# A decoder layer in split fp32: twelve of 22 feed-forward tiles go through the second weights in Strassen's form

## The chip, the cores and the metric

The kernel runs on one core of one Trainium2 chip. The metric is the device time of one execution in microseconds (us). A core has TensorE (PE) for matmuls into PSUM banks, VectorE (DVE), ScalarE (ACT) and GpSimd (POOL) for elementwise work, and SyncE (SP), whose queue issues the DMA transfers of this kernel in order.

## The reference, cut to what matters

One layer of a decoder for 1024 prompt tokens and 8 sample tokens: attention and convolution branches, their merge, then a SwiGLU feed-forward part and a gated per-layer embedding. All is float32. The change is in the feed-forward part, which computes, for the normed input h of all 1032 tokens,

```python
x = x + rms_norm(swiglu(rms_norm(x)))        # D_MODEL = 1024, D_FF = 2816
# swiglu(h): g, u = h @ w_ffn_in (1024 x 2*2816);  (silu(g) * u) @ w_ffn_out (2816 x 1024)
```

## The kernel before, in words

Activations lie transposed: features on 128 partitions, T = 1032 tokens along the free axis. D = 1024 features are KT = 8 tiles, the hidden width 2816 is NH = 22 tiles. Each float32 product is made of three matmuls: an operand is split by ScalarE, which copies it to a rounded "hi" tile, and by a subtraction that leaves the rest in a "lo" tile; `mm3` (lines 277 to 280) multiplies hi by hi, hi by lo and lo by hi into one bank. Tokens are taken in three chunks of 344 (`LC`) or in four quarters of 258 (`QN`).

The feed-forward part has two stages. The hidden stage makes tile after tile of silu(g)·u. Tiles 0 to 2 are plain products (`hidden_plain`). From tile 3 (`CLASSIC`) on it uses Strassen's form: `prepare(j)` makes sums of the four quarters of the weights on POOL and splits them, `token_sums(p)` has made four sums of quarters of h for each token half p on VectorE ahead of the stage, and a `Quad` runs seven products per token half in place of eight, in the order 1, 2, 6, 5, 7, 3, 4 (`ORDER`), over three banks. The hidden values are gathered in a slot `pk` and stored to DRAM (`d_h`), one slot and one store per tile and token half.

The second weights' stage multiplies the hidden tiles with w_ffn_out. It takes the 22 tiles in five groups, `HID = (4, 4, 3, 5, 6)`. For each group, `load_hidden` reads a tile back from `d_h` (`hr`) and splits it into `uh` (ScalarE) and `ul` (VectorE); the weights are loaded (`raw`) and split into `wh` and `wl`. For each chunk and each of the 8 output tiles f, `ffn_out` accumulates the group in one bank, and VectorE copies or adds it into `fac[f]` (`fa` in the profile). Loads for the next group go on beside the group in hand. The last group runs chunk by chunk with the final norm and the embedding behind it (`last_chain`, `p_bank`).

What sets the order: the program is written in order per engine, and a scheduler of the tile framework then moves instructions by priorities and estimated times. Tiles come from pools: `act` from 43 large slots, `raw` from 3, `sc` from 4, `rl` from 6; a tile waits until its slot's former readers are done. Banks come in turn from seven. `copies` are cache rows copied from DRAM to DRAM on SP's queue between other work. Generators that are advanced by `next(...)` between products, such as `prepare`, put side work among the matmuls.

Of the kernel before, what the change touches and what calls it, by code (L numbers as in the profile page):

```python
# [10 lines left out]
F32 = mybir.dt.float32  # L11
# [40 lines left out]
LAG = 2  # L52
TL = 2
TP = 2
HID = (4, 4, 3, 5, 6)


@with_exitstack
def decoder_step(ctx: ExitStack, tc: tile.TileContext, ins, outs):
# [24 lines left out]
    def act(s, dt=F32):  # L84
        return actp.tile([P, SLOT], dt, tag="act", name=nm(s))
# [4 lines left out]
    def rl(s):  # L90
        return rlp.tile([P, CW], F32, tag="rl", name=nm(s))
# [48 lines left out]
    def scratch(name, shape):  # L140
        return dram.tile(list(shape), F32, name=name)
# [39 lines left out]
    def w_rows(w, k):  # L181
        wq.append((w[k * P:(k + 1) * P, :].rearrange("p (f m) -> p f m", m=P), 8))
        return len(wq) - 1

    raws = {}

    def load_weight():
        j = w_emitted[0]
        src, n = wq[j]
        r = rawp.tile([P, 8 * P], F32, tag="raw", name=nm("raw"))  # L190
        SY.dma_start(r[:, :n * P].rearrange("p (k m) -> p k m", m=P), src)
        raws[j] = r
        w_emitted[0] += 1

# [22 lines left out]
    def W(i):  # L217
        return wt[i]
# [194 lines left out]
    wi_ff, h0 = [], 0  # L413
    for n_ in HID:
        wi_ff.append([w_rows(w_ffn_out, h0 + j) for j in range(n_)])
        h0 += n_
# [840 lines left out]
    def token_sums(p):  # L1257


        for j in range(4):  # L1260
            tsum[p][j] = act("th", F32R), act("tl", F32R)
        for k in range(4):
            b11, b12, b21, b22 = (m_q(f, 2 * p + h) for f in (k, k + 4) for h in range(2))
            t = [rl("t") for _ in range(4)]
            for x, a, b in ((0, b12, b11), (2, b22, b12), (1, b22, 0), (3, b21, 1)):
                V.tensor_sub(t[x][:, :QN], a, t[b][:, :QN] if isinstance(b, int) else b)
# [56 lines left out]
    prods = {}  # L1323

    def prepare(j):


        a, b = fetch(wi_st[j]), fetch(wi_st[j] + 1)
        H = 4 * P
        a1, a2, b1, b2 = a[:, :H], a[:, H:], b[:, :H], b[:, H:]  # L1330
        w = prods[j] = {}

        def split(src, hi, lo):
            A.activation(hi, src, AF.Copy)
# [10 lines left out]
        G.tensor_add(s1, b1, b2)  # L1345
        G.tensor_sub(s2, s1, a1)
# [6 lines left out]
        G.tensor_sub(s3, a1, b1)  # L1353
# [4 lines left out]
        G.tensor_sub(s4, a2, s2)  # L1358
# [11 lines left out]
    class Quad:  # L1370


        def __init__(self, j, p):
            self.j, self.p, self.t0 = j, p, 2 * p * QN
            self.banks, self.part = {}, {}
            self.pk = act("pk")

        def piece(self, i):
            return self.pk[:, i * QN:(i + 1) * QN]

        def operand(self, m, k):
            quarter = {1: (0, 0), 2: (4, 0), 3: (4, QN)}
# [15 lines left out]
        def after(self, m):
# [24 lines left out]
            else:  # L1423
                V.tensor_mul(x, ps, x)

    def hidden_strassen(j, nxt):
        for group in ((0,), (1,)) if j == CLASSIC else ((0, 1),):
            quads = []
            for p in group:
                finish(2)  # L1430
                finish(("t", p))
                quads.append(Quad(j, p))
# [6 lines left out]
            for q in quads:  # L1439
                SY.dma_start(d_h[j, :, q.t0:q.t0 + 2 * QN], q.pk[:, :2 * QN])  # L1440
        del prods[j]

    for js, qs in [(range(2), range(2)), ((2,), (0,)), (range(2), (2,)), ((2,), (1, 2))]:
        for j in js:
            ensure(wi_cl[j][1])
            for q in qs:
                hidden_plain(j, q)
    hid = {}

    def load_hidden(j):  # L1450
# [3 lines left out]
        V.tensor_sub(lo, r, hi.bitcast(F32))  # L1454
        hid[j] = hi, lo

    def first_hidden():
        for _ in range(2):
            yield
        for j in range(HID[0]):  # L1460
            ensure(wi_ff[0][j])
            yield
            load_hidden(j)
            yield

    prep = prepare(CLASSIC)
    for j in range(CLASSIC, NH):
# [10 lines left out]

    fac = [None] * KT

    def ffn_out(gi, h0, wo, f, c):
        t0, n = c
        ps = gemm_bank_rows(wo, f, [hid[h0 + k] for k in range(len(wo))], c)
        if fac[f] is None:
            fac[f] = act("fa")
        fv = fac[f][:, t0:t0 + n]
        if gi == 0:
            V.tensor_copy(fv, ps[:, :n])
        else:
            V.tensor_add(fv, fv, ps[:, :n])  # L1490

    h0 = 0
    for gi, wo in enumerate(wi_ff[:-1]):
        nj, nh = h0 + len(wo), h0 + len(wo) + len(wi_ff[gi + 1])
        nw = wo[-1] + 1
        for ci, c in enumerate(LC):
            for f in range(KT):
                ffn_out(gi, h0, wo, f, c)
                if f % 3 == 2 and nj < nh:
                    ensure(nw)  # L1500
                    load_hidden(nj)
                    nj, nw = nj + 1, nw + 1
                elif f % 4 == 3:
                    next(copies, None)
        h0 += len(wo)
    wo, gi = wi_ff[-1], len(wi_ff) - 1
    rbs = [None] * 3

    hp = [None] * 3
# [22 lines left out]
    for ci, c in enumerate(LC):  # L1532
        accs[ci] = SumSq(c)
        nf = KT - LQ if ci == 2 else KT
        for f in range(nf):
            ensure(wo[-1])
            ffn_out(gi, h0, wo, f, c)
            accs[ci].add(f, fac[f][:, c[0]:c[0] + c[1]])
            tick(2.9)
        if nf < KT:  # L1540

            t0, n = c
            pss = [bank() for f in range(nf, KT)]
            for k, wi in enumerate(wo):
                (wh, wl), (xh, xl) = W(wi), hid[h0 + k]
# [148 lines left out]
```

## Time and profile before

| | |
|---|---|
| three runs | 1713.76, 1708.15, 1712.81 us |
| median | 1712.81 us |
| the profiled execution's own time | 1709.87 us |
| its span, first to last instruction | 1708.1 us |
| mean granted TensorE clock | 0.997 |
| hidden stage, Strassen tiles (3 to 21) | about 936 to 1335 us of the span |
| second weights' stage with its last group | about 1340 to 1590 us |

In rows of the profile, a line such as "fa<-fa,g 128x344" names the written tile, the read tiles and the shape; g is a PSUM bank. All elementwise work stands under L120, a helper that records it, so it is told apart by tile names. Two times beside a row of the timeline are its start and its duration in us; square brackets hold how long the engine sat idle before it and what ended that. Matmul rows overlap: the time that one takes from the engine is the distance from start to start.

### The profile page before, as it was taken

To read this page: it belongs to the slowest core of one execution; us is meant where nothing else is said; L and a number is where in the kernel's file an instruction comes from. 1 tells how busy PE (TensorE), PEld (TensorE's weight loads), DVE (VectorE), ACT (ScalarE), POOL (GpSimd) and SP (SyncE) were. 2 spreads that over 40 slices of the span, in tenths; PEclk is the share of its full clock that TensorE was granted. 3 is DMA by queue.
4 is the path that set the end of the run, shared out by engine and by line. 5 is a ranking of instruction groups with operands and counts; after the bars stand their busy time and mean duration, and the time that the engine had idled before them with its cause. 6 is when DMAs were issued, how large, how long until landed. Compare 5 with 4: busy or idle time off the path is not lost.

```text
span 1708.1 us, 28632 instructions
## 1 busy us (share of the span) xinstructions
PE 1681.4 (98%) x11651; PEld 1653.5 (97%) x11651; DVE 1036.4 (61%) x1742; ACT 634.0 (37%) x1307; POOL 288.9 (17%) x223
## 2 busy tenths in 40 slices
PE   8999999999999999999999999999999999999999
PEld 7999999999999999999999989999999999999998
DVE  7899879958979677553789312222212445637863
ACT  6434445444442344223544333333333311213520
POOL 1000000000000000000004666766664000000000
PEclk9999999999999999999999999999999999999999
DMA  5242121121254355323331222333333523420411
GB/s 190 64 124 66 43 67 57 49 82 62 89 180 156 112 179 157 106 81 107 127 117 42 73 87 87 100 117 103 109 99 124 186 108 103 171 96 13 149 59 46
DMA packets 80890, 174.65 MB, mean 102 GB/s; under 512 B 11154, under 2 KB 49890, under 8 KB 80374
## 3 DMA queue, kind: packets, MB, share of 16 engines
q1 hardware_dynamic: 80566, 172.69, 31.0%
q8 instruction: 91, 1.49, 0.4%
q0 software_dynamic: 192, 0.13, 0.1%
q14 instruction: 41, 0.34, 0.1%
HBM read 136.16 MB, written 50.13 MB: 109 GB/s over the span
## 4 chain that ended last, share of the span: by engine, by line
PE 88%; DVE 6%; issue 2%; DMA 1%; ACT 1%; POOL 1%; SPq 0%; POOLq 0%; DVEq 0%; ACTq 0%
PE g L278 28%; PE g L280 28%; PE g L279 28%; DVE y L120 3%; PE O L675 1%; PE S L630 1%; PE PT L657 1%; DVE tl L120 1%; DVE t L120 1%; DMA d_h<-pk 1%; DVE wl L120 1%; POOL s L120 0%; DMA hr<-d_h 0%; PE m L337 0%; PE m L325 0%
## 5 line engine op out<-in xcount | busy, mean ns | idle before, releaser
L278 PE MATMUL g<-hh,wh 128*128 128x384 f32 (+1 forms) x1200 | 393.3, 328 | 7.1 <-ACT wh L120 7.1
L280 PE MATMUL g<-hh,wl 128*128 128x384 f32 (+1 forms) x1200 | 384.5, 321 | 0.3 <-DVE wl L120 0.3
L279 PE MATMUL g<-hl,wh 128*128 128x384 f32 (+1 forms) x1200 | 384.1, 320 | 0.0
L120 DVE SCALAR_TENSOR_TENSOR y<-z,taps,y 128x1023 f32<-128x1023 f32 (+14 forms) x240 | 304.0, 1267 | 36.7 <-ACT y L120 31.1
L278 PEld LDWEIGHTS g<-hh,wh 128*128 128x128 f32 x1200 | 226.6, 189 | 14.4 <-ACT wh L120 7.1
L279 PEld LDWEIGHTS g<-hl,wh 128*128 128x128 f32 x1200 | 226.4, 189 | 0.6 <-DVE hl L120 0.3
L280 PEld LDWEIGHTS g<-hh,wl 128*128 128x128 f32 x1200 | 226.0, 188 | 0.8 <-DVE wl L120 0.8
L279 PE MATMUL g<-ul,wh 128*128 128x344 f32 x528 | 169.4, 321 | 0.0
L280 PE MATMUL g<-uh,wl 128*128 128x344 f32 x528 | 168.7, 321 | 0.0
L278 PE MATMUL g<-uh,wh 128*128 128x344 f32 x528 | 162.2, 321 | 3.3 <-ACT uh L120 3.3
L120 DVE TENSOR_TENSOR wl<-raw,wh 128x1024 fp32r<-128x1024 f32 x106 | 129.1, 1222 | 35.6 <-ACT wh L120 28.7
L120 POOL TENSOR_TENSOR r<-r,mhalf 128x3 f32<-128x3 f32 x18 | 16.4, 910 | 752.8 <-DVE r L120 752.7
L120 ACT ACTIVATE wh<-raw 128x1024 fp32r<-128x1024 f32 x106 | 110.7, 1050 | 8.0 <-PE g L279 3.8
L278 PE MATMUL g<-mh,wh 128*128 128x344 f32 x336 | 107.6, 323 | 0.8 <-ACT mh L120 0.8
L120 DVE TENSOR_TENSOR pk<-p,g 128x258 f32<-128x258 f32 x76 | 31.0, 421 | 126.5 <-PE g L280 97.8
L279 PE MATMUL g<-ml,wh 128*128 128x344 f32 x336 | 107.1, 320 | 0.0
L280 PE MATMUL g<-mh,wl 128*128 128x344 f32 x336 | 107.0, 320 | 0.0
L278 PEld LDWEIGHTS g<-uh,wh 128*128 128x128 f32 x528 | 98.2, 189 | 3.6 <-ACT uh L120 3.6
L279 PEld LDWEIGHTS g<-ul,wh 128*128 128x128 f32 x528 | 99.7, 189 | 0.4 <-DVE ul L120 0.4
L120 DVE TENSOR_TENSOR p<-p,g 128x258 f32<-128x258 f32 x38 | 16.1, 425 | 138.1 <-ACT p L120 77.2
L280 PEld LDWEIGHTS g<-uh,wl 128*128 128x128 f32 x528 | 99.7, 189 | 0.0
L120 DVE TENSOR_TENSOR fa<-fa,g 128x344 f32<-128x344 f32 x96 | 47.1, 511 | 78.3 <-PE g L280 77.9
(236 smaller groups left out, 4034.1 us busy)
## 6 DMA issues: line engine op xcount, KB each, us to landing
raw<-in_w_in_dram SPq DMA_DIRECT2D x50, 512.0 KB
raw<-in_w_ffn_in_dram SPq DMA_DIRECT2D x44, 512.0 KB
hr<-d_h SPq DMA_DIRECT2D x22, 516.0 KB
raw<-in_w_ffn_out_dram SPq DMA_DIRECT2D x22, 512.0 KB
d_h<-pk SPq DMA_DIRECT2D x38, 258.0 KB
out_kvs_dram<-in_cache_kv_w_dram SPq DMA_DIRECT2D x16, 510.0 KB
d_x<-mo SPq DMA_DIRECT2D x24, 172.0 KB
out_yT_dram<-fa SPq DMA_DIRECT2D x24, 172.0 KB
```

The lines of the kernel that those rows point to most:

```text
L120: ins = fn(*a, **k)
L278: TE.matmul(ps, hi_w, xh, start=first, stop=False, skip_group_check=more)
L279: TE.matmul(ps, hi_w, xl, start=False, stop=False, skip_group_check=more)
L280: TE.matmul(ps, lo_w, xh, start=False, stop=last, skip_group_check=more)
L630: TE.matmul(sp[h][:, o:o + nk], qT[h * 64:(h + 1) * 64, blk * P:(blk + 1) * P], kT[h * 64:(h + 1) * 64, (blk + 1) * P - nk:(blk + 1) * P], ...
L657: TE.transpose(ps[:, o:o + P], e[:, o:o + P], ident)
L675: TE.matmul(ps[h * 64:(h + 1) * 64, i * P:(i + 1) * P], vtok[:, k0:k0 + 64], self.p[half][:, o:o + P], start=kb == kbs[0], stop=kb == kbs[-1])
```

## The change

Tiles 0 to 3 and 16 to 21 stay plain in the second stage. Tiles 4 to 15 become six pairs; in a pair the two tiles are the two halves of the sum index. The two token quarters of a token half and the two halves of the output rows are the other halves, so a pair takes seven products of 258 columns in place of eight. Two pairs (`PER`) are summed in a bank before it is added to the `fa` tiles that the product goes into; VectorE adds the running bank after each product, in place of a copy per part.

- Weights: `w_pair` loads one half of the output columns for both tiles of a pair, with two transfers. `mix_weights` makes four sums and all splits' subtractions on POOL: 16 instructions for a half of two pairs. In the stage of before POOL has no work.
- Hidden values: `hidden_store` makes, after each odd tile, four sums per token half on VectorE (`ts`) and stores the seven operands' sources to a new DRAM scratch `d_s`. `mix_hidden` reads them back (two transfers per pair and token half) and splits them: ScalarE the hi part, VectorE the subtractions (7 for two pairs).
- `pk` is now one slot per tile for both token halves, held until the pair is stored.
- The first part's banks are moved to `fa` by ScalarE, not VectorE.
- In the hidden stage `token_sums` makes three split sums, not four. The fourth overwrites a quarter of `mo` and is split later into `h2` by `fourth_sums`. The preparation of tile 3 has its sums and subtractions on VectorE, not POOL. The last tile is run one token half after the other.

```diff
-HID = (4, 4, 3, 5, 6)
+PLAIN0, PAIRS, PER = 4, 6, 2
...
-        for j in range(4):
+        for j in range(3):
             tsum[p][j] = act("th", F32R), act("tl", F32R)
...
+                if x == 3:
+                    V.tensor_sub(b12, a, b)
+                    continue
+                V.tensor_sub(t[x][:, :QN], a, b)
...
+    def fourth_sums(p):
+        for k in range(4):
+            src = m_q(k, 2 * p + 1)
+            hi, lo = (y[:, (2 * p + 1) * QN:(2 * p + 2) * QN] for y in h2[k])
+            A.activation(hi, src, AF.Copy)
+            V.tensor_sub(lo, src, hi.bitcast(F32))
+            yield 0.35
...
     def prepare(j):
+        E = V if j == CLASSIC else G
...
-            G.tensor_sub(lo, src, hi.bitcast(F32))
+            E.tensor_sub(lo, src, hi.bitcast(F32))
...
+    def hidden_store(j, p):
...
+        i, e = divmod(j - PLAIN0, 2)
+        d = d_s[i, p]
+        if e == 0:
+            SY.dma_start(d[:, 4 * QN:5 * QN], pk[:, t0:t0 + QN])
+            return
+        SY.dma_start(d[:, 5 * QN:], pk[:, t0:t0 + 2 * QN])
...
+        V.tensor_sub(t1, b12, b11)
+        V.tensor_sub(t2, b22, t1)
+        V.tensor_sub(t3, b22, b12)
+        V.tensor_sub(t4, b21, t2)
+        SY.dma_start(d[:, :4 * QN], ts)
...
-        for group in ((0,), (1,)) if j == CLASSIC else ((0, 1),):
+        for group in ((0,), (1,)) if j in (CLASSIC, NH - 1) else ((0, 1),):
...
-            V.tensor_copy(fv, ps[:, :n])
+            A.activation(fac[f][:, t0:t0 + n], ps[:, :n], AF.Copy)
...
+    def mix_weights(g, half):
...
+            split(a1, *direct[0], G)
+            split(r[:, 2 * H:], *direct[1], G)
+            yield
+            G.tensor_add(s1, b1, b2)
+            G.tensor_sub(s2, s1, a1)
+            split(sa, hi[:, :2 * H], lo[:, :2 * H], G)
+            yield
+            G.tensor_sub(s3, a1, b1)
+            G.tensor_sub(s4, a2, s2)
+            split(sb, hi[:, 2 * H:4 * H], lo[:, 2 * H:4 * H], G)
...
+    def mix_hidden(g, p):
+        rest = [act("ux", F32R) for _ in range(3)]
+        for e in range(PER):
+            d = d_s[g * PER + e, p]
+            rb, rt = act("hr"), act("hr")
+            SY.dma_start(rb[:, :3 * QN], d[:, 4 * QN:])
+            SY.dma_start(rt, d[:, :4 * QN])
...
+    class OutQuad:
...
+        def product(self, m):
...
+            for e in range(PER):
...
+                mm3(ps, QN, wh, wl, xh, xl, e == 0 and m in OPENS, e == PER - 1, m not in OPENS)
+            c = {1: self.c11, 2: self.c11, 6: self.c12, 3: self.c12, 5: self.c22, 7: self.c22, 4: self.c21}[m]
+            V.tensor_add(c, c, ps)
...
+            ahead = [mix_hidden(g, 1), mix_weights(g + 1, 0), mix_hidden(g + 1, 0), mix_weights(g + 1, 1)]
...
+        for (p, half), nxt in zip(((0, 0), (0, 1), (1, 0), (1, 1)), ahead):
+            for _ in pre:
+                pass
+            pre = nxt
+            quads = [OutQuad(g, p, half, i) for i in range(2)]
+            for m in ORDER:
+                for q in quads:
+                    q.product(m)
+                    next(pre, None)
```

The new part runs as twelve blocks of 84 matmuls, called B0 to B11: three groups of two pairs, in each group the blocks (token half 0, output half 0), (0, 1), (1, 0), (1, 1). `split` in the new functions is a hi copy on ScalarE and a subtraction on the engine given last (G is POOL, V is VectorE).

Three places show how the instructions now stand. First VectorE in the second stage. Before, in the first group, copies of finished banks alternate with splits for the next group:

```order
L120 COPY fa_13981<-g_13968 128x344
L120 COPY fa_13996<-g_13983 128x344
L120 TENSOR_TENSOR wl_14001<-raw_13829,wh_14000 128x1024
L120 COPY fa_13966<-g_14099 128x344
L120 TENSOR_TENSOR ul_14006<-hr_14004,uh_14005 128x1032
L120 COPY fa_14023<-g_14010 128x344
L120 COPY fa_14039<-g_14026 128x344
```

After, at the end of B1 and the start of B2 (ux and usl are the splits that B2 needs, hr what was read back):

```order
L120 TENSOR_TENSOR fa_14142<-fa_14142,g_14588 128x258
L120 TENSOR_TENSOR fa_14164<-fa_14164,g_14610 128x258
L120 TENSOR_TENSOR ux_14465<-hr_14467,ux_14464 128x774
L120 TENSOR_TENSOR usl_14490<-hr_14468,ush_14489 128x516 x2
L120 TENSOR_TENSOR ux_14465<-hr_14502,ux_14464 128x258
L120 TENSOR_TENSOR ux_14466<-hr_14502,ux_14466 128x516
L120 TENSOR_TENSOR fa_14010<-fa_14010,g_14734 128x258
L120 TENSOR_TENSOR fa_14039<-fa_14039,g_14749 128x258
L120 TENSOR_TENSOR fa_14010<-fa_14010,g_14759 128x258
L120 TENSOR_TENSOR usl_14525<-hr_14503,ush_14524 128x516 x2
```

Five splits stand directly behind B1's last adds, and two more behind the third add of B2.

Second, POOL at the same place, where it had no row before; these belong to the weights of B4 and B6 (sums sa and sb, splits wx):

```order
L120 TENSOR_TENSOR sa_14604<-raw_14261 128x256
L120 TENSOR_TENSOR sb_14605<-raw_14261 128x256
L120 TENSOR_TENSOR sa_14604<-sa_14604,raw_14261 128x256
L120 TENSOR_TENSOR sb_14605<-raw_14261,sa_14604 128x256
L120 TENSOR_TENSOR sa_14647<-raw_14322 128x256
L120 TENSOR_TENSOR sb_14648<-raw_14322 128x256
L120 TENSOR_TENSOR sa_14647<-sa_14647,raw_14322 128x256
L120 TENSOR_TENSOR sb_14648<-raw_14322,sa_14647 128x256
L120 TENSOR_TENSOR wx_14597<-raw_14261,wx_14596 128x256
```

POOL now has a row of 16 such instructions for every half of two pairs, one after the other.

Third, VectorE ahead of the hidden stage's tile 3, among the sums for token half 1 (t, tl). Before:

```order
L120 TENSOR_TENSOR t_9308<-mo_7705 128x258
L120 TENSOR_TENSOR t_9310<-mo_7709,mo_7705 128x258
L120 TENSOR_TENSOR tl_9221<-t_9268,th_9220 128x258
L120 TENSOR_TENSOR t_9309<-mo_7709,t_9308 128x258
L120 TENSOR_TENSOR tl_9215<-t_9308,th_9214 128x258
```

After, at the end of the same sums, with the preparation of tile 3 (s, wal, wbl) among them:

```order
L120 TENSOR_TENSOR mo_7706<-mo_7710,t_9234 128x258
L120 TENSOR_TENSOR t_9273<-mo_7707 128x258
L120 TENSOR_TENSOR wal_9399<-raw_9019,wah_9398 128x1024
L120 TENSOR_TENSOR tl_9175<-t_9273,th_9174 128x258
L120 TENSOR_TENSOR t_9275<-mo_7711,mo_7707 128x258
L120 TENSOR_TENSOR t_9274<-mo_7711,t_9273 128x258
L120 TENSOR_TENSOR wbl_9407<-s_1258_9403,wbh_9406 128x512
```

The instructions wal, wbl and s stood in POOL's row before; the fourth sum is written into mo and its split has left this place.

More of the change, by code (lines that the diff above doesn't have):

```diff
@@ L183, in w_rows, with w_pair @@
         return len(wq) - 1
+    def w_pair(w, ks, half):
+        srcs = [w[k * P:(k + 1) * P, :].rearrange("p (b h c) -> p b h c", b=2, h=2)[:, :, half] for k in ks]
+        wq.append((srcs, None))
+        return len(wq) - 1
     raws = {}
@@ L412, in decoder_step @@
         w_cols(w_ffn_in, DFF + j * P)
[L413 to L416, printed above, removed]
+    pairs = [(PLAIN0 + 2 * i, PLAIN0 + 2 * i + 1) for i in range(PAIRS)]
+    LAST0 = PLAIN0 + 2 * PAIRS
+    wi_ff = {j: w_rows(w_ffn_out, j) for j in range(PLAIN0)}
+    wi_fs = {}
+    for g in range(0, PAIRS, PER):
+        for half in range(2):
+            for i in range(g, g + PER):
+                wi_fs[i, half] = w_pair(w_ffn_out, pairs[i], half)
+    for j in range(LAST0, NH):
+        wi_ff[j] = w_rows(w_ffn_out, j)
     wi_P = [w_cols(w_ple_gate, i * P) for i in range(NPG)]
@@ L1344, in prepare @@
         s1, s2 = sc("s1"), sc("s2")
-        G.tensor_add(s1, b1, b2)
-        G.tensor_sub(s2, s1, a1)
+        E.tensor_add(s1, b1, b2)
+        E.tensor_sub(s2, s1, a1)
         w[6], w[5] = halves(act("wbh", F32R), act("wbl", F32R))
@@ L1424, in after @@
                 V.tensor_mul(x, ps, x)
+    packs = {}
+    def hidden_store(j, p):
+        t0 = 2 * p * QN
+        pk = packs[j]
+        if not PLAIN0 <= j < LAST0:
+            SY.dma_start(d_h[j, :, t0:t0 + 2 * QN], pk[:, t0:t0 + 2 * QN])
+            return
[3 more added lines that the diff above has]
+            SY.dma_start(d[:, 4 * QN:5 * QN], pk[:, t0:t0 + QN])
+            return
+        SY.dma_start(d[:, 5 * QN:], pk[:, t0:t0 + 2 * QN])
+        b11, b12, b21, b22 = (y[:, t0 + o:t0 + o + QN] for y in (packs[j - 1], pk) for o in (0, QN))
+        ts = act("ts")
+        t2, t1, t3, t4 = (ts[:, q * QN:(q + 1) * QN] for q in range(4))
+        V.tensor_sub(t1, b12, b11)
[3 more added lines that the diff above has]
+        SY.dma_start(d[:, :4 * QN], ts)
     def hidden_strassen(j, nxt):
-        for group in ((0,), (1,)) if j == CLASSIC else ((0, 1),):
+        pk = packs[j] = act("pk")
+        for group in ((0,), (1,)) if j in (CLASSIC, NH - 1) else ((0, 1),):
             quads = []
@@ L1438, in hidden_strassen @@
                     next(nxt, None)
-            for q in quads:
-                SY.dma_start(d_h[j, :, q.t0:q.t0 + 2 * QN], q.pk[:, :2 * QN])
+            for p in group:
+                hidden_store(j, p)
         del prods[j]
@@ L1447, in decoder_step @@
                 hidden_plain(j, q)
+    for p in range(2):
+        chains.append([fourth_sums(p), 0, ("u", p)])
     hid = {}
@@ L1455, in load_hidden, with plain_hidden @@
         hid[j] = hi, lo
+    def plain_hidden(js):
+        for j in js:
+            ensure(wi_ff[j])
+            yield
+            load_hidden(j)
+            yield
     def first_hidden():
@@ L1459, in first_hidden @@
             yield
[L1460 to L1464, printed above, removed]
+        yield from plain_hidden(range(PLAIN0))
     prep = prepare(CLASSIC)
@@ L1489, in ffn_out @@
         else:
+            fv = fac[f][:, t0:t0 + n]
             V.tensor_add(fv, fv, ps[:, :n])
[L1492 to L1505, printed above, removed]
@@ L1506, in decoder_step, with split @@
-    wo, gi = wi_ff[-1], len(wi_ff) - 1
+    wmix, xmix = {}, {}
+    def split(src, hi, lo, E, parts=1):
+        n = src.shape[1] // parts
+        A.activation(hi, src, AF.Copy)
+        for i in range(parts):
+            a = slice(i * n, (i + 1) * n)
+            E.tensor_sub(lo[:, a], src[:, a], hi[:, a].bitcast(F32))
+    def mix_weights(g, half):
+        H = 2 * P
+        rest = [act("wx", F32R) for _ in range(3)]
+        for e in range(PER):
+            r = fetch(wi_fs[g * PER + e, half])
+            a1, b1, a2, b2 = (r[:, i * H:(i + 1) * H] for i in range(4))
+            hi, lo = act("wsh", F32R), act("wsl", F32R)
+            sa, sb = sc("sa"), sc("sb")
+            s2, s1, s3, s4 = sa[:, :H], sa[:, H:], sb[:, :H], sb[:, H:]
+            if e == 0:
+                direct = [(rest[0][:, :H], rest[1][:, :H]), (rest[0][:, H:3 * H], rest[1][:, H:3 * H])]
+            else:
+                direct = [(rest[0][:, 3 * H:4 * H], rest[1][:, 3 * H:4 * H]), (rest[2][:, :2 * H], rest[2][:, 2 * H:4 * H])]
+            split(a1, *direct[0], G)
+            split(r[:, 2 * H:], *direct[1], G)
+            yield
+            G.tensor_add(s1, b1, b2)
+            G.tensor_sub(s2, s1, a1)
+            split(sa, hi[:, :2 * H], lo[:, :2 * H], G)
+            yield
+            G.tensor_sub(s3, a1, b1)
+            G.tensor_sub(s4, a2, s2)
+            split(sb, hi[:, 2 * H:4 * H], lo[:, 2 * H:4 * H], G)
+            w = wmix[g, half, e] = {1: direct[0]}
+            w[2], w[4] = (tuple(y[:, i * H:(i + 1) * H] for y in direct[1]) for i in range(2))
+            for i, m in enumerate((6, 5, 7, 3)):
+                w[m] = hi[:, i * H:(i + 1) * H], lo[:, i * H:(i + 1) * H]
+            yield
@@ new lines, in mix_hidden @@
+    def mix_hidden(g, p):
[5 more added lines that the diff above has]
+            SY.dma_start(rt, d[:, :4 * QN])
+            yield
+            if e == 0:
+                b = [tuple(y[:, i * QN:(i + 1) * QN] for y in rest[:2]) for i in range(3)]
+                split(rb[:, :3 * QN], rest[0][:, :3 * QN], rest[1][:, :3 * QN], V)
+            else:
+                b = [tuple(y[:, 3 * QN:4 * QN] for y in rest[:2])]
+                b += [(rest[2][:, i * QN:(i + 1) * QN], rest[2][:, (i + 2) * QN:(i + 3) * QN]) for i in range(2)]
+                split(rb[:, :QN], *b[0], V)
+                split(rb[:, QN:3 * QN], rest[2][:, :2 * QN], rest[2][:, 2 * QN:4 * QN], V)
+            yield
+            hi, lo = act("ush", F32R), act("usl", F32R)
+            split(rt, hi, lo, V, 2)
+            x = xmix[g, p, e] = dict(zip((1, 2, 3), b))
+            for i, m in enumerate((6, 5, 7, 4)):
+                x[m] = hi[:, i * QN:(i + 1) * QN], lo[:, i * QN:(i + 1) * QN]
+            yield
@@ new lines, in decoder_step, with __init__ @@
+    class OutQuad:
+        def __init__(self, g, p, half, i):
+            self.g, self.p, self.half, self.i = g, p, half, i
+            f, t0 = half * 2 + i, 2 * p * QN
+            self.c11, self.c12, self.c21, self.c22 = (
+                fac[h][:, t0 + o:t0 + o + QN] for h in (f, f + 4) for o in (0, QN))
+            self.banks = {}
+        def product(self, m):
+            if m in OPENS:
+                self.banks[BANK[m]] = bank()[:, :QN]
+            ps = self.banks[BANK[m]]
+            for e in range(PER):
+                wh, wl = (y[:, self.i * P:(self.i + 1) * P] for y in wmix[self.g, self.half, e][m])
+                xh, xl = xmix[self.g, self.p, e][m]
+                mm3(ps, QN, wh, wl, xh, xl, e == 0 and m in OPENS, e == PER - 1, m not in OPENS)
+            c = {1: self.c11, 2: self.c11, 6: self.c12, 3: self.c12, 5: self.c22, 7: self.c22, 4: self.c21}[m]
+            V.tensor_add(c, c, ps)
@@ new lines, in then @@
+    def then(*gens):
+        for x in gens:
+            yield from x
+    G_ = PAIRS // PER
+    last = list(range(LAST0, NH))
+    pre = then(mix_weights(0, 0), mix_hidden(0, 0), mix_weights(0, 1))
+    for ci, c in enumerate(LC):
+        for f in range(KT):
+            ffn_out(list(range(PLAIN0)), f, c)
+            next(pre, None)
+            if f % 4 == 3:
+                next(copies, None)
+    for g in range(G_):
+        if g + 1 < G_:
+            ahead = [mix_hidden(g, 1), mix_weights(g + 1, 0), mix_hidden(g + 1, 0), mix_weights(g + 1, 1)]
+        else:
+            ahead = [mix_hidden(g, 1), plain_hidden(last[:1]), plain_hidden(last[1:3]), plain_hidden(last[3:5])]
+        for (p, half), nxt in zip(((0, 0), (0, 1), (1, 0), (1, 1)), ahead):
[6 more added lines that the diff above has]
+                    q.product(m)
+                    next(pre, None)
+            next(copies, None)
@@ L1507, in decoder_step @@
+    for _ in then(pre, plain_hidden(last[5:])):
+        pass
+    for _ in copies:
+        pass
+    wo = [wi_ff[j] for j in last]
     rbs = [None] * 3
@@ L1535, in decoder_step @@
         for f in range(nf):
-            ensure(wo[-1])
-            ffn_out(gi, h0, wo, f, c)
+            ffn_out(last, f, c)
             accs[ci].add(f, fac[f][:, c[0]:c[0] + c[1]])
```

40 lines of the change are left out of this document (23 added, 17 removed).

## The prediction

> **What bounds the kernel now.** I read the page first: busy shares, the 40 slices, the chain that ended last.
>
> ```profile
> span 1708.1 us, 28632 instructions
> PE 1681.4 (98%) x11651; PEld 1653.5 (97%) x11651; DVE 1036.4 (61%) x1742; ACT 634.0 (37%) x1307; POOL 288.9 (17%) x223
> DVE  7899879958979677553789312222212445637863
> POOL 1000000000000000000004666766664000000000
> PE 88%; DVE 6%; issue 2%; DMA 1%; ACT 1%; POOL 1%; SPq 0%; POOLq 0%; DVEq 0%; ACTq 0%
> ```
>
> TensorE is busy 98% of the span and 88% of the chain that ended last is matmuls, so time can come only from fewer or shorter matmuls, or from the few idle spots. POOL works in slices 22 to 31 alone, VectorE least there and at a middle share behind. Next come the stages that the change touches, in windows (the columns are PE, weight loads, VectorE, ScalarE, POOL, granted clock, DMA share, GB/s):
>
> ```profile
> 936.00:946.00 10.00, 7.27 (x46) 6.85 (x45) 8.68 (x7) 3.59 (x9) 7.60 (x5) 0.83 0.30 81
> 988.00:996.00 8.00, 3.74 (x21) 3.72 (x20) 0.42 (x1) 2.81 (x7) 4.41 (x4) 0.79 0.50 194
> 1050.00:1300.00 250.00, 250.00 (x2083) 250.00 (x2082) 52.28 (x122) 92.49 (x200) 169.54 (x122) 1.00 0.32 104
> 1336.00:1344.00 8.00, 4.72 (x19) 4.08 (x18) 3.60 (x3) 4.02 (x4) 0.00 (x0) 0.79 0.59 209
> 1385.00:1518.00 133.00, 133.00 (x847) 133.00 (x846) 62.69 (x97) 24.20 (x24) 0.00 (x0) 1.00 0.31 109
> ```
>
> The hidden stage (1050 to 1300) and the second weights' stage (1385 to 1518) run at full clock without a gap. Three spots lose time: 936, 988 and 1336, where PE is idle 2.7, 4.3 and 3.3 us and the clock is then below 1. At 256 to 258 columns in the hidden window a matmul takes 250/2083 = 0.1200 us; in the other window, where all are 344 wide, 133/847 = 0.1570, and single starts confirm 0.158:
>
> ```profile
> 1403.83 0.32 PE L280 MATMUL g<-uh,wl 128*128 128x344 f32 x1
> ...
> 1408.88 0.32 PE L279 MATMUL g<-ul,wh 128*128 128x344 f32 x1
> ```
>
> Between these two lie 32 starts: 5.05/32 = 0.1578. I take 0.1575.
>
> **The columns.** Twelve tiles, 8 output rows, 3 chunks, 3 products each: 864 matmuls of 344 go, 864 x 0.1575 = 136.1 us. Added are 6 pairs x 2 token halves x 4 output rows of a half x 7 products x 3 = 1008 of 258, 1008 x 0.1200 = 121.0 us. Gain 15.1 us: seven eighths of the columns, less what the shorter instruction costs more per column. TensorE was at 100% in both windows, so all of it is on the path, if the new operands are there in time.
>
> The Trainium skill ("TensorE: Matmul & The Clock Gate", Back-to-back issue gap) says that streams of weight load and matmul settle near 81 ns at 128 columns and 131 ns at 512. A line through these, an estimate, gives 98 ns at 258 and 110 at 344: 95.0 us removed, 98.8 added, a loss of 3.7 us. The rows above (120 and 157.5 ns) disagree with it.
>
> **VectorE in the new stage.** One block is one token half and one half of the output rows: 84 matmuls, 10.1 us; there are 12 (B0 to B11). These rows price what stands beside it:
>
> ```profile
> L120 DVE TENSOR_TENSOR fa<-fa,g 128x344 f32<-128x344 f32 x96 | 47.1, 511 | 78.3 <-PE g L280 77.9
> L120 DVE TENSOR_TENSOR wl<-raw,wh 128x1024 fp32r<-128x1024 f32 x26 | 31.6, 1220 | 0.0
> L120 DVE TENSOR_TENSOR ul<-hr,uh 128x1032 fp32r<-128x1032 f32 x22 | 27.0, 1229 | 15.8 <-ACT uh L120 15.8
> L120 DVE COPY fa<-g 128x344 f32<-128x344 f32 x24 | 11.6, 513 | 20.4 <-PE g L280 20.3
> L120 POOL TENSOR_TENSOR wal<-raw,wah 128x1024 fp32r<-128x1024 f32 x19 | 46.0, 2421 | 28.1 <-ACT wah L120 20.6 <-PE g L280 7.5
> L120 POOL TENSOR_TENSOR s<-raw 128x512 f32<-128x512 f32 x19 | 24.5, 1288 | 18.2 <-issue 17.7 <-DMA raw<-in_w_ffn_in_dram 0.5
> L120 DVE TENSOR_TENSOR pk<-p,g x50: 409/424/426, 1053.1 to 1295.7; 128x258 f32<-128x258 f32 x50
> L120 DVE TENSOR_TENSOR pk<-pk,p x24: 427/428/847, 1064.1 to 1288.5; 128x258 f32<-128x258 f32 x24
> ```
>
> Removed: 72 adds of 344 (36.8 us), 24 copies (12.3, now ScalarE's), 12 wl (14.6), 12 ul (14.7). Added: 12 blocks x 14 adds x 0.424 = 71.2 us, and the splits of the sums read back. From 344 to 1032 columns VectorE grows by 1.04 ns a column over 0.155, so 516 costs 0.69 and 774 0.96 (estimates), and the seven splits of one `mix_hidden` 4.8 us, 29 for six. In two blocks (20.2 us) VectorE then has 28 x 0.424 + 4.8 = 16.7 us, 83%; in the window of before it had 62.69 of 133, 47%. That alone fits. What doesn't show in this sum is POOL.
>
> POOL had nothing in this stage; `mix_weights` gives it 16 instructions per half of two pairs. From 512 (1.29) and 1024 (2.42) a column costs 2.2 ns, so 256 wide is 0.73: ten of these and six of 1.29 make 15.1 us, in every 20 us block pair: 75%. And this is how a VectorE subtraction from two SBUF operands fares beside POOL (start, duration):
>
> ```profile
> 923.23 2.61 POOL L120 TENSOR_TENSOR wal<-raw,wah 128x1024 fp32r<-128x1024 f32 x1 [20.63 <-ACT wah L120]
> 923.51 2.62 DVE L120 TENSOR_TENSOR t<-mo,t 128x258 f32<-128x258 f32 x1
> 926.05 0.41 DVE L120 TENSOR_TENSOR t<-mo 128x258 f32<-128x258 f32 x1
> 939.94 4.02 DVE L120 TENSOR_TENSOR tl<-t,th 128x258 fp32r<-128x258 f32 x2
> 1103.62 1.29 POOL L120 TENSOR_TENSOR s<-raw,s 128x512 f32<-128x512 f32 x1
> 1104.43 0.76 DVE L120 TENSOR_TENSOR pk<-pk,p 128x258 f32<-128x258 f32 x1 [0.49 <-ACT pk L120]
> ```
>
> The first ends 0.29 us after the POOL instruction beside it, instead of after 0.41; the one at 1104.43 ends 0.28 after its neighbour (1103.62 + 1.29). So VectorE waits for the running POOL instruction and takes some 0.28 more. With one operand in PSUM it doesn't: fifty pk<-p,g run 409 to 426 ns with POOL at 68% (169.54 of 250). The adds into fa read PSUM, so they are safe; the splits are not. The Trainium skill ("GPSIMD Engine Reference", Key points) names the same: POOL shares its SBUF interfaces with VectorE, in contention with instructions of two SBUF inputs. By it the rival below would decide; the trace agrees on the mechanism, and no run yet shows its price here.
>
> Price of a split's wait: 0 when POOL is idle; 0.1 on average in the steady hidden stage; a whole POOL instruction, 0.94 on average, when both are back to back. At 75% share and arbitrary arrival I take 0.5, so 3.5 us per `mix_hidden`: 20.2 of 20.2. VectorE becomes saturated but not over, and what is late is decided by order. A late add costs PE nothing until its bank comes round again, some 1.7 us (7 banks, 3 per quad), so I count splits in front of a block that needs them:
> - B2. VectorE's order has five splits of the second token half (774, 516, 516, 258, 516: 3.45 us) right behind B1's last add, and B2 needs their result. PE has some 2 to 3 us of hi products to go on with. Without POOL 1.3 us idle; with a whole POOL instruction at each, 6.3. POOL's order has the sixteen for B4 just there: I take 5.
> - B4: the last two splits stand behind its first two adds: 1 (0 to 3). The three `mix_hidden` after that lie one to two blocks ahead: 1 each, 3 (0 to 9).
> - B0: first operands are made under the 45 us of plain tiles: 0.5 (0 to 3). Last plain tiles: 12 splits of 1.23 in B9 to B11, three just behind B11: 1.5 (0 to 4).
> Sum 11, bounds 3 and 25.
>
> ScalarE (24.20 of 133 us) takes the 24 evacuations, about 0.5 each, and hi copies of some 5 us per block pair: hidden. DMA: per pair and token half 0.92 MB are stored and read where 0.53 were; weights come in two 256 KB transfers for one of 512. Some 10 MB more at a DMA share of 0.31: hidden in bandwidth, and latency is covered by the two blocks that the loads stand ahead.
>
> **The hidden stage.** At 936, PE waits for VectorE, which is behind with the sums of h2 because each waits for POOL's preparation of tile 3 (4.02 us for two, above). Moved to VectorE, that preparation costs it 1.22 + 9 x 0.69 = 7.4 us, less 8 splits now made later (2.7), and takes away 16 us of waits between 896 and 944 (each such row's excess over 0.42 summed, an estimate). VectorE then ends before 936, when PE arrives. Gain at most 4.4 us (2.7 idle, the rest low clock: 10 x 0.17); worst zero, if POOL's preparation of tile 4 takes its place. I take 4.4. At 988 the chain is this:
>
> ```profile
> 985.92 0.90 SPq L120 DMA_DIRECT2D d_h<-pk  x2
> 990.80 1.15 ACT L120 ACTIVATE wbh<-s 128x512 fp32r<-128x512 f32 x2 [8.04 <-DMA d_h<-pk]
> ```
>
> ScalarE waits 8.04 us for the slot of a pk whose store left SP at 985.92, behind a weight load that waited for POOL. It costs 4.3 idle plus clock, 5.6. One pk instead of two and eight slots fewer for the sums ease this: 3 (0 to 5.6). The stall at 1336 (loads behind the last pk stores on SP) has the same order after: 0 (-2 to +2).
>
> Added: per pair 8 subtractions of 258 with two SBUF operands behind each odd tile, 0.34 to 1.3 each, and SP's store waits for them with weight loads queued behind it. VectorE has 52 of 250 us here, so it is mostly covered; an add that comes late by over 2.9 us stalls. I take 2 over six pairs (0 to 6). `fourth_sums` (8 splits) is due only at the seventh product, 8.6 us on: 0.
>
> **Sum**, against the profiled execution's 1709.87 (span 1708.1): -15.1 - 4.4 - 3 + 2 + 11 = -9.5, 1700.4. That execution lies 2.9 us below the median of 1712.81, so a median may lie a little above: 1701. A measurement tells 0.3%, 5.1 us, from no change.
>
> **Rivals.**
> - Well covered: stalls in the new stage only 3. 1709.9 - 15.1 - 7.4 + 2 + 3 = 1692. For it: the scheduler put most splits a block ahead. Against: the B2 rows. 0.20.
> - VectorE, held by POOL, is the bound in the new stage (other side). With a whole POOL instruction and 0.28 at each split (9 us for seven), two blocks take VectorE 25.7 us for PE's 20.2. Five such boundaries x 5.5 = 27 us, plus about 1.7 us each at low clock behind a stall, as at 936: 36. 1709.9 - 15.1 - 7.4 + 2 + 36 = 1725. It makes the kernel slower than the median from 23 us on, by 0.3% from 29. For it: 4.02 us for two at 939.94. Against: the steady stage's median of 428 ns, and POOL pauses a quarter of the time. 0.18, spread from 1708 to 1725.
> - The start's two stalls stay, moved to another wait: 1700.4 + 7.4 = 1708. For it: slots and SP's order there are nearly as before. 0.14.
> - A fixed cost of each matmul eats the columns: the count rises by 144, and if 258 wide came at 136.1/1008 = 0.135 in this stage, nothing is left of the 15.1: 1715.5. Against: the hidden stage's rows, which also change weights at every matmul and run at 0.120. 0.02. The Trainium skill's rule on the issue gap, above, is this rival's.
> - That the change doesn't do what it says: 864 against 1008 matmuls stand in PE's order, so this is out.
>
> **Numbers.** The likeliest case (0.46) has its own range 1695 to 1708. Faster by 0.3% (below 1707.7): 0.42 of the likeliest, 0.20 covered, 0.05 of the start's: 0.67. Slower (above 1717.9): 0.12 of VectorE's, 0.01 of the start's, 0.02 of the others: 0.15. The rest 0.18. The range 1689 to 1717 leaves some 0.05 below, in the covered case with POOL's waits near zero, and 0.14 above.
>
> **What would show it.** Right: 1008 matmuls g<-ush or ux of 258 at 0.120; the window of a steady pair of blocks 20 us; PE's waits in the new stage summing to about 11, most at B2 on VectorE's usl or ux; splits of 0.69 drawn out to over 1 us; 936 to 946 at clock 1. Wrong: adds into fa that last longer than 0.43 beside POOL; PE idle before B4, B6, B8 each by over 5 us; waits on DMA for hr or raw in the new stage; a spacing of 258 other than 0.120.

## The result and the profile after

The changed kernel takes 1703.13 us in the median of five runs (1698.74 to 1703.4), the kernel before 1712.85 in five (1708.15 to 1713.76): a ratio of 0.994, 95% interval 0.9922 to 0.9959. It is 9.7 us faster; 1701 was forecast. Its profiled execution is the quickest of its five, at 1698.74 us.

The page of the changed kernel, the lines that answer to those of before:

```profile
span 1697.0 us, 29372 instructions
PE 1666.4 (98%) x11795; PEld 1636.1 (96%) x11795; DVE 1111.9 (66%) x1890; ACT 664.5 (39%) x1385; POOL 378.3 (22%) x309
DVE  7899879958979676553689344333322258867853
POOL 1000000000000000000002767666672549400000
PE 87%; DVE 7%; issue 2%; ACT 1%; DMA 1%; POOL 0%; SPq 0%; POOLq 0%; DVEq 0%; ACTq 0%
```

There are 144 matmuls more, and TensorE is busy for 15.0 us less; 4.7 of these are the side edits' own (1676.7 in experiment 1). VectorE is busy for 75 us more and POOL for 89, and POOL's work now reaches on through slices 32 to 35. What PE waits for, by releaser (total us, times, longest), from 925 to 1345 us, before and then changed, and last the changed kernel from 1345 to 1512:

```profile
PE g L278 <- ACT p L120: 7.0, 3, 4.3
PE g L278 <- ACT uh L120: 3.3, 1, 3.3
...
PE g L288 <- DVE pk L120: 5.4, 4, 1.4
PE g L288 <- ACT uh L120: 3.1, 1, 3.1
...
PE g L288 <- DVE fa L120: 4.9, 5, 2.5
PE g L289 <- DVE ux L120: 1.7, 4, 0.6
```

The waits at 936 and 988 (ACT p, 7.0) are gone. In their place stand four waits of some 1.34 us for VectorE's pk, and in the new stage waits for fa and ux. The one at the start of the second stage (uh) stayed. Windows of the changed kernel, with the columns of the prediction's windows:

```profile
936.00:946.00 10.00, 10.00 (x86) 10.00 (x85) 3.55 (x7) 3.99 (x10) 9.58 (x8) 1.00 0.12 45
1060.00:1080.00 20.00, 18.66 (x155) 18.45 (x155) 11.52 (x17) 6.11 (x14) 11.79 (x9) 1.00 0.29 98
1385.00:1470.00 85.00, 78.68 (x629) 76.01 (x629) 71.57 (x135) 34.63 (x57) 67.79 (x65) 1.00 0.54 184
1474.00:1502.00 28.00, 28.00 (x236) 28.00 (x235) 24.45 (x49) 7.03 (x7) 0.00 (x0) 1.00 0.45 151
```

936 to 946 is now full at clock 1. In the blocks, 236 matmuls in 28 us are 0.119 each where POOL does nothing; from 1385 to 1470, where POOL is busy 80%, there are 629 where 85/0.120 = 708 would fit. Now the stages, as distances between the first matmuls of each in the timelines of the profiled executions. "Side edits" is the first experiment below, which has no Strassen form in the second stage; "repeat" is the changed kernel profiled again.

| us | before | changed | repeat | side edits |
|---|---|---|---|---|
| hidden, plain tiles (from 859.8) | 75.8 | 73.2 | 73.4 | 73.9 |
| hidden, Strassen tiles | 394.1 | 389.6 | 389.7 | 383.9 |
| second stage in all | 257.8 | 253.4 | 257.2 | 258.5 |
| of it the twelve blocks, to the first plain matmul behind | | 130.2 | 131.8 | |
| of it all 1008 matmuls of the blocks, plain ones taken off | | 131.7 | 133.2 | |
| from there to the end | 116.5 | 116.5 | 116.7 | 116.3 |

The first row of the blocks ends 12 matmuls early, because three plain ones stand among the last of B11; the second counts all 1008 and takes off 0.1575 us for each plain one. Of the gain, 7.1 us lie ahead of the second stage and 4.4 in it (0.6 in the repeat), and the last column asks whether the Strassen form brought any of it.

### The profile page after: what moved, and what is told of

It is laid out like the page before. It is cut to its first block, busy times and chain, and to the rows that moved or that the text cites. A ratio compares the mean times of both kernels' runs of the same rounds, so it can differ in the third digit from the quotient of the medians.

```text
span 1697.0 us, 29372 instructions
## 1 busy us (share of the span) xinstructions
PE 1666.4 (98%) x11795; PEld 1636.1 (96%) x11795; DVE 1111.9 (66%) x1890; ACT 664.5 (39%) x1385; POOL 378.3 (22%) x309
## 4 chain that ended last, share of the span: by engine, by line
PE 87%; DVE 7%; issue 2%; ACT 1%; DMA 1%; POOL 0%; SPq 0%; POOLq 0%; DVEq 0%; ACTq 0%
PE g L288 28%; PE g L289 28%; PE g L290 27%; DVE y L120 3%; DVE ts L120 1%; PE O L691 1%; PE S L646 1%; PE PT L673 1%; DVE pk L120 1%; DVE usl L120 1%; DVE wl L120 1%; DMA raw<-in_w_in_dram 0%; PE m L347 0%; DMA hr<-d_h 0%; PE m L335 0%
## 5 line engine op out<-in xcount | busy, mean ns | idle before, releaser
L120 DVE TENSOR_TENSOR wl<-raw,wh 128x1024 fp32r<-128x1024 f32 x94 | 114.9, 1226 | 34.6 <-ACT wh L120 28.8
L120 ACT ACTIVATE wh<-raw 128x1024 fp32r<-128x1024 f32 x94 | 98.2, 1052 | 8.8 <-PE g L289 3.8
L120 DVE TENSOR_TENSOR fa<-fa,g 128x258 f32<-128x258 f32 (+1 forms) x192 | 77.5, 430 | 35.6 <-PE g L290 34.0
L120 ACT ACTIVATE p<-g 128x258 f32<-128x258 f32 x114 | 43.4, 383 | 125.0 <-PE g L290 125.0
L288 PE MATMUL g<-mh,wah 128*128 128x258 f32 x304 | 86.5, 284 | 5.4 <-DVE pk L120 5.4
L120 ACT ACTIVATE sg<-g 128x384 f32<-128x384 f32 (+1 forms) x68 | 30.9, 455 | 145.9 <-PE g L290 123.4
L288 PE MATMUL g<-th,wbh 128*128 128x258 f32 x304 | 86.0, 283 | 0.0
L289 PE MATMUL g<-ml,wah 128*128 128x258 f32 x304 | 86.0, 283 | 0.0
```

Of the source, the lines that this page charges most:

```text
L120: ins = fn(*a, **k)
L288: TE.matmul(ps, hi_w, xh, start=first, stop=False, skip_group_check=more)
L289: TE.matmul(ps, hi_w, xl, start=False, stop=False, skip_group_check=more)
```

## The experiments

**1. Which part of the change carries the gain.** The kernel before with the edits around hidden tile 3 alone:

```diff
 # before.py
+        E = V if j == CLASSIC else G      # prepare(): tile 3 on VectorE
-        for j in range(4):                # token_sums(): three split sums,
+        for j in range(3):                # the fourth later, by fourth_sums()
```

> The kernel before with only the edits around hidden tile 3: its preparation on VectorE, three split sums with the fourth split later into h2. The second weights' stage stays plain. Theory A, that these edits carry the gain: the hidden plain part ends 2.6 us sooner, the 4.4 us lost at 936 are gone, the 5.6 at 988 go or stay: 7 to 12.6 us faster than before, 1700 to 1706. Theory B, that the Strassen form of the second stage carries it: within 2 us of before, 1711 to 1714, with PE idle at 936 and 988 as before.

Measured: 1698.9 us against 1712.34 of the kernel before, ratio 0.9921 (0.9904 to 0.9937). It was run a second time, beside the kernels of the last experiment:

> The kernel before with the side edits around hidden tile 3 only (no Strassen form in the second stage), on the chip of the two runs beside it: 1697 to 1700. If the Strassen form is worth nothing as long as POOL and VectorE share the stage, it lies within 2 us of the changed kernel with its sums on POOL.

Measured: 1698.46 against 1711.79, 0.992 (0.9905 to 0.9935). Theory A holds, and the gain is larger than its 7 to 12.6 us: without the Strassen form of the second stage the kernel is some 4 us faster than with it. The runs with it stood on other chips; by the ratios to the kernel before on each chip the difference is 3 us for the first pair of runs, whose intervals overlap, and 6 for the second pair, whose intervals are apart. PE's waits from 925 to 1345 in experiment 1:

```profile
PE g L278 <- ACT uh L120: 3.5, 1, 3.5
PE g L278 <- ACT p L120: 0.4, 1, 0.4
PE g L279 <- DVE ul L120: 0.2, 1, 0.2
```

Of the stalls on p only 0.4 us is left, and the hidden stage's 383.9 us are its 19 x 168 matmuls at 0.120 (383.0) with 0.9 added.

**2. Undoing one of the side edits.**

```diff
 # after.py
-        E = V if j == CLASSIC else G
+        E = G
```

> The changed kernel with the preparation of hidden tile 3 back on POOL; PE's order is the same. If VectorE's waits for POOL there cost the stalls of 936: VectorE rows of over 1 us come back between 920 and 945, PE loses 4 to 7 us, 1707 to 1710. Rival, that the missing fourth sums (8 splits and their slots) took the stalls away: within 2 us of the changed kernel, 1701 to 1705.

Measured: 1711.25 us against 1712.34, ratio 0.9993 (0.9984 to 1.0003). One line takes the whole gain back, 1 us more than the expectation allowed. The hidden plain part grew from 73.2 to 80.7 us and the rest of the hidden stage from 389.6 to 394.1. The longest of PE's waits there, two places of VectorE (timeline: start, duration), and a window:

```profile
905.84 0.66 PE L290 MATMUL g<-mh,wl 128*128 128x344 f32 x1 [4.19 <-DVE wl L120]
...
929.18 2.97 DVE L120 TENSOR_TENSOR tl<-t,th 128x258 fp32r<-128x258 f32 x2
940.35 4.33 DVE L120 TENSOR_TENSOR ml<-mo,mh 128x258 fp32r<-128x258 f32 x3
...
984.00:1000.00 16.00, 16.00 (x135) 16.00 (x135) 3.39 (x9) 5.62 (x12) 7.87 (x6) 1.00 0.21 68
```

Two and three subtractions of 0.42 take 2.97 and 4.33 us. The ml are the fourth sums' splits. The window shows that the stall of 988 did not come back with POOL's preparation: PE is full there.

**3. The same edit alone**, `E = V` in the kernel before with its four split sums:

> The kernel before with one edit only, the preparation of hidden tile 3 on VectorE in place of POOL (four split sums as before). Theory: this line carries most of what the side edits bring, because without POOL VectorE's sums no longer wait: 936 and 988 lose nothing, 1699 to 1702. Rival: without the removed fourth sums VectorE still comes late by the 2.7 us of eight splits plus the 7.4 us that it took over: 1704 to 1708.

Measured: 1704.83 us against 1711.0, ratio 0.9963 (0.9949 to 0.9977). It recovers half, less than the theory expected and within the rival's range. One stall stays, at 989 us, the longest of the waits on p:

```profile
PE g L278 <- ACT p L120: 6.0, 3, 4.6
...
984.00:1000.00 16.00, 11.44 (x83) 11.23 (x82) 1.70 (x4) 4.79 (x12) 9.54 (x9) 0.89 0.27 104
```

So the two edits act mainly on different stalls. The preparation on VectorE ends PE's waits ahead of 936 and halves those on p around it (2.7 to 1.4 us). The stall at 988 goes with the fourth split sums: the kernels with four have it (before, experiment 3), those with three do not (changed, experiments 1 and 2), whichever engine prepares tile 3. Experiment 1 differs from this one in the fourth sums alone; experiment 2 also has the Strassen form and its other pk slots. Whether the freed slots or the order on SP's queue does it was not told apart.

**4. POOL taken out of the second stage.**

```diff
 # after.py, mix_weights
-            G.tensor_add(s1, b1, b2)
+            A.activation(s1, b1, AF.Copy)
...                                        # likewise s2, s3, s4 and the four lo parts
```

> The changed kernel with every POOL instruction of mix_weights replaced by a ScalarE copy of the same shape, so the sums and lo parts of the mixed weights are left out. Theory, VectorE held by POOL: splits ux and usl fall to 0.42 to 0.96 us each, PE's loss in the twelve blocks falls from 11 us to 4 or less, 1695 to 1697. Rival, VectorE's order and load alone: the stalls before B2 and B6 stay within 2 us of what they were, 1701 to 1704. ScalarE at 38% plus about 40% should not become a bound; if it does, PE waits on ACT.

Measured: 1692.35 us, ratio 0.9879 to before (0.9864 to 0.9893), 10.8 us below the changed kernel (10 to 13 by the ratios, on different chips). PE's waits from 1345 to 1512 and a window of this kernel; then the usl rows of first the changed kernel and then this one (times of one: shortest, median, longest, ns); last, the adds into fa in the blocks of the changed kernel:

```profile
PE g L289 <- DVE ux L120: 0.4, 1, 0.4
PE g L288 <- DVE fa L120: 0.3, 1, 0.3
...
1385.00:1470.00 85.00, 84.34 (x701) 83.93 (x700) 65.31 (x150) 60.04 (x121) 0.00 (x0) 1.00 0.53 183
...
L120 DVE TENSOR_TENSOR usl<-hr,ush x22: 681/970/1802, 1376.0 to 1475.2; 128x516 fp32r<-128x516 f32 x22
L120 DVE TENSOR_TENSOR usl<-hr,ush x22: 687/690/692, 1377.6 to 1471.4; 128x516 fp32r<-128x516 f32 x22
...
L120 DVE TENSOR_TENSOR fa<-fa,g x168: 406/423/427, 1375.0 to 1505.1; 128x258 f32<-128x258 f32 x168
```

There are 701 matmuls in place of 629, and the 1008 of the blocks last 122.3 us in place of 131.7 (121.0 by the sum). VectorE's five splits still stand right behind B1's last add, as in the changed kernel, and B2 loses 1.2 us in place of 3.3. Order and load alone are not the cause; waiting for POOL is. The adds into fa, which read a PSUM bank, are not held: none of the 168 lasts over 0.427 us. In the changed kernel the longest single wait was in B6; VectorE, POOL and PE there:

```profile
1439.31 2.94 DVE L120 TENSOR_TENSOR usl<-hr,ush 128x516 fp32r<-128x516 f32 x2
1439.98 1.71 POOL L120 TENSOR_TENSOR wx<-raw,wx 128x512 fp32r<-128x512 f32 x1
1442.63 0.39 PE L288 MATMUL g<-ux,wx 128*128 128x258 f32 x1 [2.50 <-DVE fa L120]
```

Two splits that take 1.30 alone take 2.94 beside POOL, the adds behind them come late, and PE has no bank for 2.50 us. POOL is slowed as well: its split of 512 columns takes 1.71 here, where the prediction's rows had 1.29 for that width.

**5. The sums in the hidden stage.** Left out first (copies by ScalarE in their place), then moved to POOL, which computes all:

```diff
 # after.py, hidden_store; 4 lines alike
-        V.tensor_sub(t1, b12, b11)
+        A.activation(t1, b12, AF.Copy)    # experiment e4
+        G.tensor_sub(t1, b12, b11)        # experiment e7
```

> The changed kernel with the four sums of hidden_store as ScalarE copies of one of their operands (the sums are left out); stores and loads are unchanged. Theory, the sums wait for POOL on VectorE and delay the product that frees a bank: the four waits of PE of 1.34 us at 1078 to 1204 are gone, 5.4 us faster than the changed kernel, 1697 to 1699. Rival, the longer stores or the pk slots cause them: they stay, 1702 to 1704.

> The changed kernel with the four sums of hidden_store on POOL, which has 30% idle in the hidden stage. Theory that these sums hurt only by waiting on VectorE: hidden stage 383.5 to 385 in place of 389.6 us, 1697 to 1699. Rival: POOL, with 3 us more per tile, prepares the next tile late or its waits come back through SP's store: hidden stage 388 or more, 1702 to 1706.

> The changed kernel itself once more, on the chip of the runs beside it, as their measure: 1701 to 1704, with the stages as before: hidden 389 to 390 us, twelve blocks 130 to 132.

Measured: 1695.51 us without them (0.99, 0.9885 to 0.9914), 1697.57 on POOL (0.9919, 0.9904 to 0.9934), and the changed kernel again 1702.48 (0.9953, 0.9938 to 0.9967). The hidden stage takes 383.3, 383.6 and 389.7 us. The changed kernel's timeline and its chain of waits, at one of the four places:

```profile
1071.51 2.64 POOL L120 TENSOR_TENSOR wal<-raw,wah 128x1024 fp32r<-128x1024 f32 x1 [6.72 <-ACT pk L120]
1072.14 2.30 DVE L120 TENSOR_TENSOR ts<-pk,pk 128x258 f32<-128x258 f32 x1
1078.60 0.39 PE L288 MATMUL g<-mh,wah 128*128 128x258 f32 x1 [1.34 <-DVE pk L120]
...
by line: DVE ts L120 47.5%; DVE pk L120 32.2%; PE g L288 7.5%; PE g L290 5.0%; ACT pk L120 4.3%; PE g L289 3.6%; issue 1.4%
```

From 1070 to 1080 the chain runs through ts for 47.5%: one ts of 0.42 lasts until the POOL instruction beside it ends (1074.15) and 0.29 more. The product pk that frees the bank queues behind. On POOL the sums cost the hidden window nothing, changed and then with the sums on POOL:

```profile
1050.00:1300.00 250.00, 244.64 (x2031) 243.82 (x2031) 84.19 (x155) 87.18 (x190) 162.20 (x116) 1.00 0.34 112
1050.00:1300.00 250.00, 249.97 (x2083) 249.76 (x2082) 64.45 (x127) 87.98 (x194) 184.08 (x148) 1.00 0.35 116
```

2083 matmuls again, as before the change.

**6. The cache copies.** Two copies of 510 KB stand on SP's queue ahead of what B2 reads back; this one has none between plain tiles and B11:

```diff
 # after.py
-            if f % 4 == 3:
-                next(copies, None)
...
-            next(copies, None)            # after each block
```

> The changed kernel with no cache copies between the plain tiles and the blocks; those left go out behind B11. If the stall at B2 comes from hr landing late behind two 510 KB copies on SP's queue: the splits for B2 start about 5 us sooner, 1.5 to 2.5 us of the block losses go, 1700 to 1702. Rival, that VectorE's waits for POOL set it all the same: blocks still 130 to 132 us, 1702 to 1704, or later where the copies now delay the last plain tiles' loads.

Measured: 1735.59 us, slower by 1.0143 (1.0128 to 1.0158). The blocks took 130.4 us by the table's first row for them, as much as ever, so the copies are not their stall. The cost came behind them; PE's waits from 1345 to 1640, a window, and VectorE's first residual adds in this kernel and then in the changed one:

```profile
PE m L335 <- DVE acc L120: 13.7, 1, 13.7
PE g L288 <- ACT wh L120: 11.4, 3, 9.9
PE g L288 <- DVE fa L120: 9.2, 9, 2.4
...
1530.00:1566.00 36.00, 36.00 (x234) 35.97 (x233) 11.95 (x25) 1.48 (x3) 0.86 (x1) 1.00 0.00 1
...
1577.94 1.37 DVE L120 TENSOR_TENSOR fa<-fa,res 128x344 f32<-128x344 f32 x3
...
1535.44 0.94 DVE L120 TENSOR_TENSOR fa<-fa,res 128x344 f32<-128x344 f32 x2
```

The norms and the embedding behind the blocks waited, but not for the transfers themselves: from 1530 to 1566 the DMA engines move next to nothing and VectorE is busy for only 12 of 36 us. What changed is VectorE's order: the adds of the residual (res), whose loads SP issued from 1520 on, behind the copies, now stand behind the last group's adds and start at 1577.94 in place of 1535.44. The norm's sums (acc) follow them, and PE waits 13.7 us. Why the scheduler set this order was not tested.

**7. A better version.** With the sums on POOL, `usl` is split by one subtraction of 1032 columns in place of two, so there are fewer occasions to wait; and, as the other way, the splits of the second token half are on POOL:

```diff
 # after.py with ts on POOL
-            split(rt, hi, lo, V, 2)
+            split(rt, hi, lo, V)          # experiment e9
+            split(rt, hi, lo, G if p else V, 2)   # experiment e10, with the two rb splits alike
```

> The changed kernel with the sums of hidden_store on POOL, and the 1032 columns of usl split by one subtraction in place of two of 516: five splits per two pairs that can wait for POOL, not seven. Theory, each wait costs about a POOL instruction: two fewer for each of five token halves in the blocks, 2 to 4 us less loss there than with POOL sums alone, 1693 to 1696. Rival: one instruction of 1.23 us holds the adds behind it longer than their 1.7 us of slack allows, no change, 1697 to 1699.

> The changed kernel with the sums of hidden_store on POOL and the splits of the second token half (those of B2, B6 and B10) on POOL as well, so that VectorE has only the adds there. Theory, the waits between the two engines are what costs: adds stay at 0.42, the stalls at B2 and B6 shrink, 1694 to 1697. Rival: POOL takes 1.29 for 516 columns where VectorE takes 0.69, and the splits stand behind the weights' sums in its order: B2 and B6 wait longer for POOL than they did for VectorE, 1698 to 1704.

Measured: one split 1691.67 us, ratio 0.9877 to before (0.9863 to 0.9892), the fastest that computes all; splits on POOL 1699.53 (0.9926, 0.9909 to 0.9942). In the first the 1008 matmuls of the blocks take 126.7 us, where they took 132.1 with the sums on POOL alone (experiment 5); 665 matmuls stand from 1385 to 1470, and the waits in the stage are small. In the second, the blocks take 135.6 us and two long waits are left (2.87 us in B3 and 4.30 in B7). The rows of the first, then of the second:

```profile
PE g L288 <- DVE fa L120: 2.3, 4, 1.2
PE g L289 <- DVE usl L120: 0.5, 1, 0.5
PE g L289 <- DVE ux L120: 0.5, 2, 0.4
...
L120 DVE TENSOR_TENSOR usl<-hr,ush x11: 1224/1309/1659, 1373.5 to 1467.1; 128x1032 fp32r<-128x1032 f32 x11
...
PE g L288 <- DVE fa L120: 8.7, 5, 4.3
L120 POOL TENSOR_TENSOR usl<-hr,ush x12: 1296/1303/1341, 1389.2 to 1473.5; 128x516 fp32r<-128x516 f32 x12
```

One subtraction of 1032 columns has a median of 1.31 us, 0.09 over its shortest; two of 516 had 1.94 by their median in the changed kernel and 1.60 in its repeat. On POOL a split of 516 takes 1.30 to 1.34 every time, behind the weights' sums, and PE waits up to 4.3 us. With the one split and the sums on POOL the Strassen form gains: 1691.67 against 1698.46 of the side edits alone, on the same chip. With the sums on POOL and the splits left in two it is worth nothing yet: 1697.57 (0.9919) against those 1698.46 (0.992).

## Why the prediction was right, and where only its sum was

The forecast of 1701 stands 2 us from the median, and the sum of 1700.4 1.7 us from the execution profiled. Term by term, in that execution:

- Columns, -15.1. Right: 0.119 to 0.120 us a matmul at 258 columns, and the blocks take 122.3 us with POOL away. The line from 81 to 131 ns that the Trainium skill ("TensorE: Matmul & The Clock Gate", Back-to-back issue gap) gives is refuted here: 1008 matmuls at 98 ns would be 98.8 us. (At 344 columns that line gives 109 ns, not the 110 of the prediction; its loss would be 4.4 us.)
- Stalls in the new stage, 11. The size was right: 131.7 - 121.0 = 10.7 (12.3 in the repeat). The cause was right too (experiment 4). The places were not. A block of 84 matmuls without a loss takes 10.1 us from its first matmul to the next block's; B2 was given 5 and lost 3.3, B6 was given 1 and lost 2.8, B8 was given 1 and its splits cost 2.0 in B7, where they stand. B6's last two splits stand at its own start and not a block ahead. The prediction judged these splits by whether their block needs them soon, and left out the adds that queue behind them.
- 936, -4.4. Right: 936 to 946 is full, and undoing the line brings waits back (experiment 2). Beyond that the plain part ended 2.6 us sooner, which the sum did not have, since the waits from 896 on were counted only as VectorE's.
- 988, -3 within 0 to 5.6. It came to the whole 5.6; it went with the fourth split sums (experiments 2 and 3).
- Sums in the hidden stage, +2 within 0 to 6. Mis-sized: 5.7 us (389.6 against 383.9). The step that failed set the slack of 2.9 us against single sums of at most 1.3. Eight of them stand in a row with the products that free the banks, each can wait for POOL, and one took 2.30; a wait of that length, 2.62 for one subtraction, was already in the row at 923.51.
- 1336, 0: its wait is 3.1 after 3.3.

The measured terms add up to -11.3 where the sum had -9.5: 988 and the plain part gave 5.2 more than forecast, the hidden sums took 3.7 more and the blocks 0.3 less. That the total came so near is in part luck, and a split by parts shows what it hid: the Strassen form by itself was forecast at -15.1 + 11 + 2 = -2 us, and it costs some 4: 1703.13 and 1702.48 with it (0.994 and 0.9953 of the kernel before), 1698.9 and 1698.46 without (0.9921 and 0.992). The stage table says where: 5.7 us more in the hidden stage, and in the second stage 5.1 less in one profile and 1.3 in the other. The three terms measured give +1.3 in the first and +2.9 in the repeat, whose plain tiles ahead of the blocks also take 2.2 longer. The gain of the whole is the side edits', 13.4 us where the sum had 7.4.

VectorE held by POOL, the rival of the other side, was the right mechanism at a lesser price: 10.7 us in the blocks where it would have needed 29 to make the kernel slower by 0.3%. The rule behind it in the Trainium skill ("GPSIMD Engine Reference", Key points) agrees with experiment 4, and the runs now put the price to it: 10.8 us here, and 6 to 8 at hidden tile 3 (experiments 3 and 2).

## What to carry to other kernels

Before work goes to an idle POOL, look for subtractions and sums of two SBUF operands that VectorE makes meanwhile: each may wait for a whole POOL instruction, as the one of 2.30 us did, and what queues behind it waits too. Adds with a PSUM operand ran beside POOL at their usual 0.42 us. Where both engines had to be used, one long instruction on VectorE lost less than two short ones (experiment 7). A change of several parts should be timed part by part: here the headline part lost 4 us, and two small edits beside it gained 13.

## What the runs showed that was not expected

A single line, which engine prepares one weight tile, is worth 8 us of 1703 (experiment 2). Moving cache copies that look free cost 33 us; the trace shows no late transfer behind the blocks, but VectorE's work there in another order (experiment 6). And a matmul can wait 2.50 us for its bank although neither VectorE nor POOL is full over the stage: from 1385 to 1470 VectorE is busy 84% and POOL 80%. A good part of what VectorE shows as busy is waiting: 71.57 us for 135 rows, where 65.31 for 150 did without POOL.
